# Differential attention scores: 64-row products against full-array products with zero rows

## Chip, cores and metric

The kernel runs on one core of one Trainium2 chip. The metric is the device time of one execution in microseconds (us), the median of several runs. TensorE (PE) does the matrix products, ScalarE (ACT) and VectorE (DVE) the work between them, GpSimd (POOL) small vector steps and fills, and the SP queue issues the transfers.

## The reference

One layer of a hybrid encoder block: 256 tokens, model width 2048, everything in float32. A projection feeds an mLSTM group (4 heads) and a differential attention group (8 heads); their outputs go through one output projection, and a SwiGLU feed-forward follows. Three modulation vectors per half come from `silu(c) @ w_ada`. The part that the change touches is this:

```
s = einsum('bhmqd,bhmkd->bhmqk', qb, kb) * DA_DH ** -0.5      # m: two maps of d = 64 each
allowed = k_chunk <= q_chunk                                   # chunks of 64 tokens
p = softmax(where(allowed, s, -inf))
a = p[:, :, 0] - lam * p[:, :, 1]                              # then a @ v, v of 128 per head
```

It is done in blocks of 128 queries: block 0 sees 128 keys, block 1 sees 256. Only the diagonal 128 x 128 part of a block has masked entries: its first 64 queries don't see its last 64 keys.

## The kernel before

The main stream is a list of ticks. A tick is 256 rows of K by 512 columns of a weight matrix for all 256 tokens: 12 products of 512 columns in `product` (lines 568 to 570), since each f32 operand is split into a high and a low part (`weights_hi` on ACT makes wh two ticks ahead, `weights_lo` on DVE makes wl). The raw weights come in three buffers of 1 MB, w_ada in four of 512 KB, both issued on the SP queue when a buffer comes free. The w_in sweeps come first, then w_out (wo), w_gate_up (gu) and w_down (dn).

Everything else is background work: Python generators that a planner (`Plan`) runs step by step between half ticks, in the order in which they were added, as far as free PSUM banks (four) and the booked load of DVE and ACT permit (no further step in this half tick once one of them is booked over 2.3 us). So the order of the instructions on every engine is fixed when the program is made. Its small f32 products all go through `mm` (line 216), its transposes through `tr` (line 220), ACT's instructions through `act` (line 211).

The steps around the change. `prep` (lines 715 to 746) makes the transposed q or k of four heads: squares, the norm (sclq or rstk, on DVE and, by `rsqrt_newton`, POOL lines 387 to 390), rotary products, 8 transposes into two PSUM banks, and the copy to a tile of a pool of 31 slabs (128 x 1024 f32): qT or kT, where the partitions 0 to 63 hold map 0 and 64 to 127 map 1. `attend` (lines 752 to 796), for each head: four score products with 64 partitions each, every one followed by a product of an identity matrix with the 128-column mask bmask (bf16) that adds -1e30 to the masked entries; then row maxima on DVE (line 769), a scaling on POOL (line 771), the exponentials on ACT, the difference of the two maps on DVE, transposes. `attend_values` and `finish_attention` follow. `ml_scores` (lines 910 to 958) is the same kind of step of the mLSTM group: products L and qk of 128 partitions, with a mask product of the same form. `ada_use` issues the products gv for the modulation.

Of the kernel before, what the change touches and what calls it, by code (L numbers as in the profile page):

```python
# [12 lines left out]
BF16 = mybir.dt.bfloat16  # L13
# [5 lines left out]
P = 128  # L19
D = 2048  # L20
NEG = -1.0e30
# [59 lines left out]
class Work:  # L81
    """Background work in steps; a step follows the one before it by at least a tick."""

# [6 lines left out]
class Plan:  # L90
    """Interleaves the steps of background work with the ticks of the main matrix products."""

# [72 lines left out]
def tile_block(ctx, tc, x, c, pos, par, w_ada, w_in, w_gt, w_out, w_gu, w_dn, out):  # L165
# [9 lines left out]

# [1 line left out]
    def fs(ap):  # L177
# [25 lines left out]
    def act(o, a, func, bias=None, scale=None, accum=None):  # L203
        kw = {}
        if bias is not None:
            kw["bias"] = bias
        if scale is not None:
            kw["scale"] = scale
        if accum is not None:
            kw["accum_out"] = accum  # L210
        nc.scalar.activation(o, a, func, **kw)  # L211
        n = sum(y is not None and not isinstance(y, float) for y in (bias, scale, accum))
        plan.a += fs(o) / 1200 + 0.07 + 0.09 * n
# [9 lines left out]
    def slab(name, dt=F32):  # L223
        return sl.tile([P, 1024], dt, name=name, tag="slab")
# [4 lines left out]
    def const(shape, name, dt=F32):  # L229
        return cp.tile(shape, dt, name=name)  # L230
# [3 lines left out]

# [1 line left out]
    part = const([P, NPAR - 256], "part")  # L236
# [21 lines left out]

# [1 line left out]
    ones = const([P, P], "ones")  # L260
# [13 lines left out]
    for i in range(2):  # L274
# [10 lines left out]
                            fill=NEG, base=0, channel_multiplier=1)  # L285
    bmask = const([P, P], "bmask", BF16)
    nc.gpsimd.memset(bmask[:], 0.0)
    nc.gpsimd.memset(bmask[0:64, 64:128], NEG)
    junk = const([P, 512], "junk", BF16)
# [7 lines left out]

# [1 line left out]
    items = []  # L299
# [176 lines left out]

# [1 line left out]
    ticks = []  # L478

    def visit(accname, first, last, acts, src, name, halves, ready=(), done=None):  # L480
        """halves: list of (kb, half) in the order of K; acts(kb) gives (hi, lo)."""
        for n, (kb, h) in enumerate(halves):
            ticks.append(dict(acc=accname, start=first and n == 0, stop=last and n == len(halves) - 1,
                              act=acts, kb=kb, h=h, src=src, name=name, ready=ready,
                              done=done if n == len(halves) - 1 else None, split=None, mid=None))
# [62 lines left out]
    def acc_tile(acc, k):  # L548
        """The accumulator of token tile k; those that are drained one by one have tiles of their own."""
        if acc in apart and k == 1:  # L550
            return apart[acc][:]
        return tok(accs[acc], k)
# [19 lines left out]
    def products(i, half):  # L572
        """Half of a tick; the two ticks that end a group with "split" go token tile by token tile."""
        t = ticks[i]
        if t["split"] is None:
            for k in range(2):
                product(i, half, k)
        else:
            first = i - t["split"]
            for j in range(2):  # L580
                product(first + half, j, t["split"])
        if half == 1 and t["split"] != 0:
            for n in range(i - (t["split"] or 0), i + 1):
                del wtiles[n]

# [1 line left out]
    ropet = {}  # L587
# [71 lines left out]

# [1 line left out]
    proj = {}  # L661
# [30 lines left out]

# [1 line left out]
    sclq = const([P, 2, 16], "sclq")  # L694
# [20 lines left out]
    def prep(nm, g):  # L715
        t = proj[(DQ if nm == "q" else DK)[g]]
        dst = (sclq if nm == "q" else rstk)[:, :, g * 8:(g + 1) * 8]
        tmp = sm.tile([P, 2, 16], F32, name=f"rs{nm}{g}", tag="rs", bufs=3)
        xx, b = tmp[:, :, 0:8], tmp[:, :, 8:16]
        yield 0  # L720
        sq = slab(f"sq{nm}{g}")
        act(sq[:], t[:], AF.Square)
        yield 0
        red(xx, sq.rearrange("p (t m d) -> p t m d", t=2, d=64), ALU.add)
        ts(xx, xx, 1.0 / 64, EPS, ALU.mult, ALU.add)
        rsqrt_first(dst, b, xx)
        rsqrt_newton(dst, b, xx)
        if nm == "q":
            nc.gpsimd.tensor_scalar(dst, dst, 0.125, None, op0=ALU.mult)
            rope_products(nm, t)  # L730
        else:
            yield 0
            v = t.rearrange("p (t m d) -> p t m d", t=2, d=64)
            for k in range(2):
                tt(v[:, k], v[:, k], dst[:, k].unsqueeze(2).to_broadcast([P, 8, 64]), ALU.mult)
            yield 0
            rope_products(nm, t)
        yield 2
        pts = [misc(f"tp{nm}{g}{half}") for half in range(2)]
        for half in range(2):  # L740
            transposes4(pts[half], t, half)
        yield 0
        o = (qT if nm == "q" else kT)[g] = slab(f"{nm}T{g}")
        for half in range(2):
            act(tok(o, half), pts[half][:], AF.Copy, scale=None if nm == "q" else wqk[:, 0:1])
        plan.rel(2)
# [5 lines left out]
    def attend(h):  # L752
# [3 lines left out]
        blocks = []  # L756
        for t in range(2):
            ke = 128 * (t + 1)
            for m in range(2):
                pr = slice(m * 64, m * 64 + 64)  # L760
                o = sc[m][:, t * 128:t * 128 + ke]
                mm(o, qT[g][pr, hh * 256 + t * 128:hh * 256 + t * 128 + 128], kT[g][pr, hh * 256:hh * 256 + ke],
                   True, False)
                mm(o[:, t * 128:], identb[:], bmask[:], False, True, passes=1)
                blocks.append((t, m, o))
# [78 lines left out]

# [1 line left out]
    cw = par_("cw").rearrange("p (t j) -> p t j", t=8)  # L846
# [177 lines left out]

# [1 line left out]
    def gate_rows(s, rows, name):  # L1026
# [41 lines left out]
    def turn(stage, heads):  # L1068
        """The last products of w_out and the first of w_gate_up go token tile by token tile; this is what lies between."""
        if stage == 0:  # L1070
# [31 lines left out]

# [1 line left out]
    fpart = {}  # L1104
# [74 lines left out]

# [1 line left out]
    spans = {}  # L1181
# [54 lines left out]

    # how many quarters of w_ada each span of ticks takes: (first tick, last tick, items)
    loads = []
# [13 lines left out]

# [1 line left out]
    plan.t = 3.2  # L1254
# [74 lines left out]

# [1 line left out]
    pending = []  # L1331
# [48 lines left out]
class Lazy:  # L1380
    """A generator that is made when its first step runs; that step needs no bank before it."""

# [84 lines left out]
```

## Time and profile before

| | |
|---|---|
| runs (us) | 1249.21, 1253.47, 1253.92; median 1253.47 |
| span of the profiled execution, first to last instruction | 1246.5 us (its device time is not printed) |
| mean granted TensorE clock | 0.993 |
| PE busy | 1224.0 us, 98% |
| DVE, ACT, POOL busy | 65%, 47%, 9% |
| DMA | 313.84 MB, mean 252 GB/s |
| score products (64 records) and mask products (32) of the eight heads | between 254.3 and 383.8 us |

The span is the time from the first to the last instruction of one execution. An f32 product shows as two records on PE. The end of a record is modelled, and records overlap; what a product takes of the stream is read from the start of one record to the start of the next. PEld is TensorE's weight load, PEclk the granted clock as a share of full speed.

### The profile page before, as it was taken

Reading aid. Unit: us, or ns where it says so; the run is one execution under the profiler, and the core shown is the slowest. Engines: PE = TensorE matmul, PEld = TensorE weight load, DVE = VectorE, ACT = ScalarE, POOL = GpSimd, SP = SyncE. Lnnn points to the kernel's source line nnn. Section 1 sums busy time; section 2 is a strip of 40 time slices with the busy share of each in tenths; the row PEclk is TensorE's granted clock in tenths of the full one; section 3 lists DMA queues with packets and bytes.
Section 4 is the critical chain, followed back from the end, with each engine's and each line's share of the span. In section 5 each row is a group of like instructions: output and inputs, shape, how many; then the busy total and the mean of one; then the engine's idle time right before and its main releaser. Section 6 shows DMA issues by size and latency. Waiting matters only on the chain.

```text
span 1246.5 us, 15450 instructions
## 1 busy us (share of the span) xinstructions
PE 1224.0 (98%) x5858; PEld 963.2 (77%) x5858; DVE 815.9 (65%) x1064; ACT 587.4 (47%) x817; POOL 112.2 (9%) x249
## 2 busy tenths in 40 slices
PE   6999999999999999999999999999999999999998
PEld 2667877667778788788888888888888878888886
DVE  2657976557667998777988986555445454545453
ACT  3654444446646644765434454434344443434332
POOL 1010221200302412011100000000000000000000
PEclk9999999989999999999999999999999999999999
DMA  8889997746755989698998856555555545646461
GB/s 332 300 299 349 343 377 282 281 151 249 256 219 194 330 331 353 264 341 302 354 352 332 309 181 218 201 176 200 188 183 197 183 169 195 220 169 223 165 251 54
DMA packets 63260, 313.84 MB, mean 252 GB/s; under 512 B 6993, under 2 KB 7377, under 8 KB 41169
## 3 DMA queue, kind: packets, MB, share of 16 engines
q1 hardware_dynamic: 63186, 312.86, 69.1%
q8 instruction: 46, 0.75, 0.2%
q14 instruction: 28, 0.23, 0.1%
HBM read 310.73 MB, written 2.10 MB: 251 GB/s over the span
## 4 chain that ended last, share of the span: by engine, by line
PE 95%; DMA 2%; DVE 1%; ACT 1%; issue 0%; SPq 0%; POOL 0%; ACTq 0%
PE gv L216 3%; PE sc L216 2%; DMA ada<-in_w_ada_dram 2%; PE acc('dn', 0)_8051 L570 2%; PE acc('dn', 0)_8051 L568 2%; PE acc('dn', 2)_8853 L570 2%; PE acc('dn', 2)_8853 L569 2%; PE acc('dn', 1)_8473 L570 2%; PE acc('dn', 1)_8473 L569 2%; PE acc('dn', 0)_8051 L569 2%; PE acc('dn', 2)_8853 L568 2%; PE acc('dn', 1)_8473 L568 2%; PE apart('dn', 3)_9234 L570 1%; PE apart('dn', 3)_9234 L569 1%; PE acc('dn', 3)_9233 L570 1%; PE acc('dn', 3)_9233 L569 1%
## 5 line engine op out<-in xcount | busy, mean ns | idle before, releaser
L181 DVE TENSOR_TENSOR wl<-r,wh 128x1024 fp32r<-128x1024 f32 x392 | 474.4, 1222 | 252.0 <-ACT wh L211 250.6
L211 ACT ACTIVATE wh<-r 128x1024 fp32r<-128x1024 f32 x392 | 410.3, 1058 | 414.6 <-DMA r<-in_w_gu_dram 64.7
L185 DVE SCALAR_TENSOR_TENSOR ada<-ada,silc 128x1024 f32<-128x1024 f32 x120 | 144.7, 1218 | 0.0
L376 POOL TENSOR_TENSOR modc<-part,gsum 128x2 f32<-128x2 f32 (+1 forms) x34 | 24.5, 722 | 396.5 <-DVE ada L185 277.7
L216 PE MATMUL gv<-ada,early 128*32 128x256 f32 x576 | 47.1, 420 | 4.6 <-DMA ada<-in_w_ada_dram 4.4
L216 PEld LDWEIGHTS gv<-ada,early 128*32 128x32 f32 x576 | 13.3, 112 | 30.5 <-issue 20.7
L568 PE MATMUL acc('dn', 0)_8051<-wh,aTh 128*128 128x512 f32 x88 | 35.9, 408 | 0.0
L378 POOL TENSOR_TENSOR modc<-modc,gsum 128x2 f32<-128x2 f32 (+1 forms) x58 | 30.9, 533 | 46.8 <-DVE ada L185 43.4
L570 PE MATMUL acc('dn', 0)_8051<-wh,aTl 128*128 128x512 f32 x88 | 34.3, 390 | 0.0
L569 PE MATMUL acc('dn', 0)_8051<-wl,aTh 128*128 128x512 f32 x88 | 34.3, 389 | 0.0
L568 PE MATMUL acc('dn', 1)_8473<-wh,aTh 128*128 128x512 f32 x88 | 34.2, 389 | 0.0
L569 PE MATMUL acc('dn', 1)_8473<-wl,aTh 128*128 128x512 f32 x88 | 34.2, 389 | 0.0
L570 PE MATMUL acc('dn', 1)_8473<-wh,aTl 128*128 128x512 f32 x88 | 34.2, 389 | 0.0
L568 PE MATMUL acc('dn', 2)_8853<-wh,aTh 128*128 128x512 f32 x88 | 34.2, 389 | 0.0
L569 PE MATMUL acc('dn', 2)_8853<-wl,aTh 128*128 128x512 f32 x88 | 34.2, 389 | 0.0
L570 PE MATMUL acc('dn', 2)_8853<-wh,aTl 128*128 128x512 f32 x88 | 34.2, 389 | 0.0
L181 DVE TENSOR_TENSOR hl<-hx,hh 128x512 fp32r<-128x512 f32 (+1 forms) x18 | 11.4, 632 | 26.7 <-ACT hh L211 26.6
L211 ACT ACTIVATE hx<-pt,modc,gcol 128x256 f32<-128x256 f32 (+1 forms) x36 | 17.4, 534 | 16.8 <-PE pt L220 11.7
L211 ACT ACTIVATE gr<-gv 128x256 f32<-128x256 f32 x18 | 6.9, 383 | 34.5 <-PE gv L216 34.5
L216 PE MATMUL sc<-kT,qT 64*128 64x128 f32 (+1 forms) x64 | 20.2, 397 | 0.0
L211 ACT ACTIVATE aTh<-at 128x512 fp32r<-128x512 f32 x22 | 11.9, 595 | 17.2 <-PE at L220 17.2
L569 PEld LDWEIGHTS acc('dn', 0)_8051<-wl,aTh 128*128 128x128 f32 x88 | 16.5, 188 | 4.2 <-issue 1.0
(987 smaller groups left out, 3041.6 us busy)
## 6 DMA issues: line engine op xcount, KB each, us to landing
ada<-in_w_ada_dram SPq DMA_DIRECT2D x192, 512.0 KB, 5.6
r<-in_w_gu_dram SPq DMA_DIRECT2D x76, 1024.0 KB, 5.1
r<-in_w_dn_dram SPq DMA_DIRECT2D x44, 1024.0 KB, 4.8
r<-in_w_in_dram SPq DMA_DIRECT2D x36, 1024.0 KB, 7.1
r<-in_w_out_dram SPq DMA_DIRECT2D x16, 1024.0 KB, 7.4
r<-in_w_in_dram SPq DMA_DIRECT2D x24, 512.0 KB, 5.9
r<-in_w_gu_dram SPq DMA_DIRECT2D x24, 512.0 KB, 5.2
x<-in_x_dram SPq DMA_DIRECT2D x4, 512.0 KB, 5.8
```

Source lines behind the costliest of these rows:

```text
L181: nc.vector.tensor_tensor(o, a, b, op=op)
L185: nc.vector.scalar_tensor_tensor(out=o, in0=a, scalar=s, in1=b, op0=op0, op1=op1, accum_out=accum)
L211: nc.scalar.activation(o, a, func, **kw)
L216: nc.tensor.matmul(o, l, r, start=start, stop=stop, **kw)
L376: nc.gpsimd.tensor_tensor(o, parts[0], parts[1], op=ALU.add)
L378: nc.gpsimd.tensor_tensor(o, o, y, op=ALU.add)
L568: nc.tensor.matmul(o, ah[:, s], wh[:, r], start=t["start"] and j == 0, stop=False)
L569: nc.tensor.matmul(o, ah[:, s], wl[:, r], start=False, stop=False)
L570: nc.tensor.matmul(o, al[:, s], wh[:, r], start=False, stop=t["stop"] and j == 1)
```

## The change

`bmask` becomes 256 columns wide: the 128-column mask twice. In `prep`, q is kept in two tiles, one for each map, 128 partitions each: POOL fills the other map's 64 partitions with zeros, and ACT copies the map's own 64 partitions from PSUM (four copies of 64 x 512 instead of two of 128 x 512). k stays as it is. In `attend`, one mask product of 256 columns per bank is issued first and starts the group; block 1 (256 keys) then lies in columns 0 to 255 and block 0 in columns 256 to 383 of the bank, so that the mask's columns 128 to 383 are the two diagonals. The four score products follow with all 128 partitions and add to it, block 1 first. The rest of the diff takes comments out.

```diff
-    bmask = const([P, P], "bmask", BF16)
+    bmask = const([P, 2 * P], "bmask", BF16)
     nc.gpsimd.memset(bmask[:], 0.0)
-    nc.gpsimd.memset(bmask[0:64, 64:128], NEG)
+    for y in range(2):
+        nc.gpsimd.memset(bmask[0:64, y * P + 64:y * P + 128], NEG)
...
-        o = (qT if nm == "q" else kT)[g] = slab(f"{nm}T{g}")
-        for half in range(2):
-            act(tok(o, half), pts[half][:], AF.Copy, scale=None if nm == "q" else wqk[:, 0:1])
+        if nm == "q":
+            o = qT[g] = [slab(f"qT{g}_{m}") for m in range(2)]
+            for m in range(2):
+                nc.gpsimd.memset(o[m][64 - 64 * m:128 - 64 * m, :], 0.0)
+            for half in range(2):
+                for m in range(2):
+                    r = slice(m * 64, m * 64 + 64)
+                    act(tok(o[m], half)[r], pts[half][r], AF.Copy)
+        else:
+            o = kT[g] = slab(f"kT{g}")
+            for half in range(2):
+                act(tok(o, half), pts[half][:], AF.Copy, scale=wqk[:, 0:1])
         plan.rel(2)
...
-        for t in range(2):
+        for m in range(2):
+            mm(sc[m][:, 128:384], identb[:], bmask[:], True, False, passes=1, skip_group_check=True)
+        for t, off in ((1, 0), (0, 256)):
             ke = 128 * (t + 1)
             for m in range(2):
-                pr = slice(m * 64, m * 64 + 64)
-                o = sc[m][:, t * 128:t * 128 + ke]
-                mm(o, qT[g][pr, hh * 256 + t * 128:hh * 256 + t * 128 + 128], kT[g][pr, hh * 256:hh * 256 + ke],
-                   True, False)
-                mm(o[:, t * 128:], identb[:], bmask[:], False, True, passes=1)
+                o = sc[m][:, off:off + ke]
+                mm(o, qT[g][m][:, hh * 256 + t * 128:hh * 256 + t * 128 + 128], kT[g][:, hh * 256:hh * 256 + ke],
+                   False, True, skip_group_check=True)
                 blocks.append((t, m, o))
```

## Rows read from the trace of the kernel before

**Rows 1.** The page: busy time by engine, and the chain that ended last.
```profile
PE 1224.0 (98%) x5858; PEld 963.2 (77%) x5858; DVE 815.9 (65%) x1064; ACT 587.4 (47%) x817; POOL 112.2 (9%) x249
PE 95%; DMA 2%; DVE 1%; ACT 1%; issue 0%; SPq 0%; POOL 0%; ACTq 0%
```
**Rows 2.** Stretches: length, busy PE PEld DVE ACT POOL, granted clock, DMA share, GB/s.
```profile
265.00:272.00 7.00, 7.00 (x20) 4.39 (x20) 4.64 (x14) 2.08 (x8) 1.32 (x2) 0.53 0.01 2
361.00:367.00 6.00, 6.00 (x28) 3.37 (x27) 3.72 (x10) 2.21 (x4) 0.20 (x1) 1.00 0.59 199
410.00:420.00 10.00, 9.34 (x45) 7.23 (x44) 10.00 (x17) 8.31 (x14) 0.00 (x0) 1.00 0.97 344
```
**Rows 3.** PE in order of time around head 0: start, length, what.
```profile
253.79 0.39 PE L569 MATMUL acc('in', 7, 4)_2233<-wl,hh 128*128 128x512 f32 x1
254.01 0.39 PE L570 MATMUL acc('in', 7, 4)_2233<-wh,hl 128*128 128x512 f32 x1
254.33 0.48 PE L216 MATMUL sc<-kT,qT 64*128 64x128 f32 x2
254.75 0.23 PE L216 MATMUL sc<-bmask,identb 128*128 128x128 bf16 x1
254.91 0.49 PE L216 MATMUL sc<-kT,qT 64*128 64x128 f32 x2
...
256.94 0.47 PE L568 MATMUL acc('in', 7, 4)_2233<-wh,hh 128*128 128x512 f32 x1
257.25 0.39 PE L569 MATMUL acc('in', 7, 4)_2233<-wl,hh 128*128 128x512 f32 x1
```
**Rows 4.** PE in order of time around a group of ml_scores.
```profile
324.97 0.39 PE L570 MATMUL acc('in', 4, 4)_2698<-wh,hl 128*128 128x512 f32 x1
325.20 0.59 PE L216 MATMUL L<-ml,upper 128*128 128x257 f32 x2
325.63 0.39 PE L216 MATMUL L<-ml,ones 128*128 128x129 f32 x2
325.86 0.22 PE L216 MATMUL L<-cmask,identb 128*128 128x128 bf16 x1
325.91 0.44 PE L216 MATMUL L<-ml,upper 128*128 128x129 f32 x2
...
326.25 0.87 PE L216 MATMUL qk<-cv,cv 128*128 128x128 f32 x4
326.77 0.58 PE L568 MATMUL acc('in', 4, 4)_2698<-wh,hh 128*128 128x512 f32 x1
327.19 0.40 PE L569 MATMUL acc('in', 4, 4)_2698<-wl,hh 128*128 128x512 f32 x1
```
**Rows 5.** The weight loads ahead of these two groups, in order of time.
```profile
254.33 0.29 PEld L216 LDWEIGHTS sc<-kT,qT 64*128 64x128 f32 x2 [0.35 <-ACT wh L211]
...
324.97 0.42 PEld L216 LDWEIGHTS L<-ml,upper 128*128 128x128 f32 x2
```
**Rows 6.** PE around heads 1 and 2, which run back to back.
```profile
262.03 0.48 PE L216 MATMUL sc<-kT,qT 64*128 64x128 f32 x2
...
264.76 0.48 PE L216 MATMUL sc<-kT,qT 64*128 64x128 f32 x2
...
268.80 0.78 PE L568 MATMUL acc('in', 7, 4)_2233<-wh,hh 128*128 128x512 f32 x1
...
272.31 0.39 PE L570 MATMUL acc('in', 7, 4)_2233<-wh,hl 128*128 128x512 f32 x1
```
**Rows 7.** ACT and POOL around the q copy (time order); a memset's group (busy, mean ns).
```profile
231.25 1.08 ACT L211 ACTIVATE qT<-tpq 128x512 f32<-128x512 f32 x2 [0.69 <-PE tpq L220]
233.90 1.06 ACT L211 ACTIVATE wh<-r 128x1024 fp32r<-128x1024 f32 x1 [1.56 <-issue]
...
243.14 0.21 POOL L387 TENSOR_TENSOR rsk<-rstk 128x16 f32<-128x16 f32 x1 [8.19 <-DVE rstk L192]
...
L268 POOL MEMSET early<- 128x512 f32 x1 | 0.5, 524 | 0.0
```
**Rows 8.** PE in order of time, its first products of w_ada.
```profile
12.06 2.27 PE L216 MATMUL gv<-ada,early 128*32 128x256 f32 x16 [0.95 <-DMA ada<-in_w_ada_dram]
```

## The prediction

> **What bounds the kernel now.** I read the page first. TensorE is busy 98% of the span and holds 95% of the chain that ended last [rows 1], so a microsecond taken from its stream is worth a microsecond as long as nothing else has been waiting just behind it. The stream is in program order: the main products of w_in run all the time, and the eight heads' score products are set between them, from 254 to 384 us. So I asked for the PE timeline around one head, and for comparison around a group of other small f32 products (`ml_scores`), which use all 128 rows.
>
> Between main products the start-to-start distance is 0.22 to 0.23 us [rows 3]. Head 0: the last main product before it starts at 254.01, its first score record at 254.33 (0.32, so 0.09 more than usual), the first main product after it at 256.94, the next one at 257.25 (0.31, 0.08 more than usual) [rows 3]. A head therefore puts 0.09 + 2.61 + 0.08 = 2.78 us into the stream. It holds 2 x (128 + 256) = 768 f32 columns and 4 x 128 = 512 bf16 mask columns.
>
> The comparison: 515 f32 columns for L, two 128-column masks and 384 f32 columns for qk start at 325.20, 0.23 after the main product before (no extra), the next main product starts at 326.77, and the one after it at 327.19 (0.42, 0.19 more) [rows 4]. That is 1.57 + 0.19 = 1.76 us for 899 f32 and 256 bf16 columns: more columns, a microsecond less. A mask there takes 0.05 us of the stream (325.86 to 325.91) [rows 4]; in the head, a 128-column product with its mask takes 0.58 (254.33 to 254.91) [rows 3], against 0.23 + 0.05 here. The weight loads tell why: the load for L starts at 324.97, with the product before it, 0.23 before its own; the 64-row load of a head starts at 254.33, together with its product [rows 5]. The array of the heads waits at each step between the 64-row and the 128-row form, eight times a head.
>
> The second thing in the stream is the clock. Heads 1 and 2 run back to back (262.03 and 264.76) [rows 6]. In 265 to 272 us the granted clock is 0.53 of full, so it lay at the 1.2 GHz level for nearly all of it [rows 2]; what PE did before it fell was 3 us of such head products. The other back-to-back pair, 361 to 367, kept 1.00 [rows 2].
>
> **The change part by part.** *Score products.* After the change, a head is two mask products of 256 columns and four full-array f32 products with the same 768 columns: rows of zeros cost no columns. By the comparison group: 1.76, less a 129-column product (325.63 to 325.86, 0.23), plus 256 more mask columns (2 x 0.05 = 0.10) [rows 4], makes 1.63 us. Saved per head 2.78 - 1.63 = 1.15, for eight heads 9.2 us. The bounds: at most the exit's 0.19 disappears too (1.34 a head, 10.7 us); at least each of the two masks pays the switch that a head's mask pays now, 254.75 to 254.91, 0.16 against 0.05 [rows 3, 4] (0.93 a head, 7.4 us). I take 9.2, since the comparison group has the very forms that come.
>
> Here a rule of the Trainium skill speaks against the change. The rows show 64-row products costing more than full ones [rows 3, 4]. TensorEngine Tiling, section Overview, says the opposite of half-height products: with a contraction of 64 the array can be used as two tiles, for up to twice the speed. By that, padding would give a factor away; but the same page, section Tiling Modes, says that a change of the tiling mode drains the engine, and the head changes it at every mask. The trace agrees with the second sentence; the first is a rival below.
>
> *Clock.* Head 2 took 268.80 - 264.76 = 4.04 us up to the next main product, where head 0 took 2.61 (254.33 to 256.94): 1.43 lost. The eight intervals of main products from 268.80 to 272.31 took 3.51 instead of 8 x 0.23 + 0.08 = 1.92: 1.59 lost [rows 3, 6]. Together 3.0 us. Afterwards the pair is 3.3 us of full-array products, the form of the comparison group, so I take it that this fall goes: 3.0, with bounds 0 (it falls all the same) and 6.0 (a second fall, in executions where the other pair falls too).
>
> *q kept twice.* ACT copies each half twice: two 512-column copies more per group, 1.08 us [rows 7], if 64 partitions take as long as 128. ACT stands idle 1.56 us before its next weight split at 233.90 [rows 7], which covers it for group 0; a weight split is made two ticks ahead of its products, which covers it for group 1. If both covers were gone: 2 x 1.08 = 2.2 us. The planner books about 1 us more on ACT per group and may move background steps by half a tick; the steps then meet other neighbours in the same stream, which costs or gains fractions of a us. I take nothing, and +-1 in the range.
>
> *Zero fill.* Two memsets of 64 x 1024 per group on POOL. The nearest row is 128 x 512 in 0.52 us [rows 7]; a row of twice the length makes some 1.0, 2.1 per group. They queue behind the q norm's steps and ahead of the k norm's, and POOL stands idle for 8.19 us before the latter, at 243.14 [rows 7]: hidden. PE needs the zeros only at 254.33. If that cover were gone, k's norm, its transposes and with them PE would move by 2.1 us per group. Each group also takes one more of the 31 slabs; an allocation may wait for an earlier reader. I take nothing, and 1 us in the range.
>
> *Set-up.* The mask's three memsets are longer by less than the 0.52 us of that row; PE's first products start later by this, but then wait 0.95 us for w_ada data anyway [rows 8]. Nothing. *Order of blocks.* The reductions wait for a bank's last product as now; they only come earlier.
>
> **What is late next.** After 384 us the stream is as before, 12 us earlier. DVE is the next candidate: it is busy 10.00 of 10 us in 410 to 420, where PE lost 0.66 us [rows 2]. But its load there starts with what PE delivers, and so starts earlier as well. DMA has nothing to catch up: loads are issued as buffers come free, which is earlier too.
>
> Sum: 9.2 + 3.0 = 12.2 us. The profiled execution has a span of 1246.5; its own device time is not printed. The runs are 1249.21, 1253.47 and 1253.92, so 2.7 to 7.4 lie outside that span or in executions unlike it. The sum is a difference, and I take it off the median: 1253.5 - 12.2 = 1241.3.
>
> **The rivals.** *The clock falls all the same*, there or at a new place, since the pair stays a stretch of small products. For it: it has fallen at one pair and not at the other, so it hangs on little [rows 2]. Against: no full-array stretch of small products here shows it. 1253.5 - 9.2 = 1244.3; with a further fall 1247.3, hardly to be told from no change.
> *A second fall goes*: the median run may have had one more than the profiled one (the 4.7 us between the runs leave room): 1253.5 - 15.2 = 1238.3.
> *The gain is given back*: the covers of ACT and POOL are both gone, 2.2 + 4.2 = 6.4 us: 1247.7. Against: the idle rows named above [rows 7].
> *It doesn't do what it says*: the two maps run side by side now (the rule of the Trainium skill above), and afterwards in a row. Each head would then gain nothing from the switches and stream 384 f32 columns more, at the 0.52 us of qk's 384 [rows 4]: 8 x 0.52 = 4.2 us slower, 1257.7. Against: the m = 1 product starts 0.58 us after that of m = 0, behind a mask [rows 3].
> *Slower*: a memset of the second q slab waits for that slab's last reader, and POOL, in order, holds the k norm behind it. The point is the 8.19 us of idle time at 243.14 [rows 7]: each us beyond it moves kT's transposes and with them PE. To lose 6.3 us after a gain of 12.2, the two waits must be 18.5 us beyond their cover together; at 20, 1261.3. Nothing in the profile shows a slab wait of this size on POOL.
>
> **How the numbers follow.** A measurement of this kernel can tell about 0.5%, 6.3 us, from no change. Forecast, 9 to 13 us gained: 0.58. Clock falls as before: 0.12 (1244.3), with a further fall 0.05 (1247.3). Second fall goes: 0.10 (1238.3). Given back: 0.09 (1247.7). Doesn't do what it says: 0.03. Slower: 0.03. Faster by over 6.3 (below 1247.2): 0.58 + 0.12 + 0.10 and some of the cases on the edge, 0.83. Within: 0.13. Slower: 0.04. The range: low end 1253.5 - 10.7 - 6.0 = 1236.8, with the planner's 1 us 1235.8; high end 1253.5 - 7.4 + 1 = 1247.1.
>
> **What would show it.** Right: the step from a head's first mask to the first main product after it is about 1.5 us; no extra 0.09 before it; the granted clock in 262 to 272 is 1.00; ACT and POOL rows of the fill with PE undisturbed around 231 to 254. Wrong: a record of sc with the same spacing as now, PE waiting for POOL or ACT ahead of a head, or new stretches of a clock of 0.5 between 231 and 400. The forecast fails if the spans differ by less than 9 us while the heads are as short as I say: then the gain was lost behind 384 us.

## The result, and the profile after

| | before | after |
|---|---|---|
| device time, median (us) | 1253.38 (1249.21 to 1253.92) | 1237.44 (1235.34 to 1238.58) |
| profiled execution: span (us) | 1246.5 | 1236.0 |
| mean granted TensorE clock in it | 0.993 | 0.996 |
| ratio of the times | | 0.9881, 95% interval 0.9862 to 0.9900 |

The changed kernel is 15.9 us faster. Its profiled execution took 1237.84 us, 1.84 more than its span; with the same margin the profiled execution of before took about 1248.3, well below the median of its kernel.

The page of the changed kernel, busy time by engine and the chain that ended last (before: [rows 1]):

```profile
PE 1213.9 (98%) x5842; PEld 961.8 (78%) x5842; DVE 815.3 (66%) x1064; ACT 589.2 (48%) x821; POOL 115.8 (9%) x254
PE 95%; DMA 2%; DVE 1%; ACT 1%; issue 0%; SPq 0%; POOL 0%; ACTq 0%
```

PE is busy 10.1 us less and is the bound as before. The PE timeline of the changed kernel around head 0 (start, length, what; before: [rows 3]) and around heads 1 and 2 (before: [rows 6]):

```profile
255.03 0.39 PE L571 MATMUL acc('in', 7, 4)_2239<-wh,hl 128*128 128x512 f32 x1
255.26 0.39 PE L216 MATMUL sc<-bmask,identb 128*128 128x256 bf16 x2
255.49 1.47 PE L216 MATMUL sc<-kT,qT 128*128 128x256 f32 x8
256.72 0.48 PE L569 MATMUL acc('in', 7, 4)_2239<-wh,hh 128*128 128x512 f32 x1
257.03 0.39 PE L570 MATMUL acc('in', 7, 4)_2239<-wl,hh 128*128 128x512 f32 x1
...
261.75 0.39 PE L216 MATMUL sc<-bmask,identb 128*128 128x256 bf16 x2
261.98 1.47 PE L216 MATMUL sc<-kT,qT 128*128 128x256 f32 x8
263.29 0.38 PE L216 MATMUL sc<-bmask,identb 128*128 128x256 bf16 x2
```

The first mask comes 0.23 after the main product before it, with no extra. From it to the next main product there are 1.46 us, and the main product after that starts 0.31 later, 0.08 more than usual. A head puts 1.54 us into the stream instead of 2.78; in the pair the second head starts 1.54 after the first. Saved per head: 1.24, for eight heads 9.9 us.

Three stretches of the changed kernel (length, busy PE, PEld, DVE, ACT, POOL, granted clock, DMA share, GB/s): the two pairs of heads, and the step from w_out to w_gate_up (before, the first pair: [rows 2]):

```profile
260.00:268.00 8.00, 8.00 (x43) 6.69 (x42) 5.07 (x14) 6.12 (x16) 0.80 (x2) 1.00 0.52 196
354.00:358.00 4.00, 4.00 (x25) 3.54 (x24) 3.62 (x10) 1.01 (x2) 0.41 (x2) 1.00 0.63 200
...
492.00:497.00 5.00, 4.20 (x11) 3.37 (x12) 4.02 (x10) 3.07 (x7) 0.00 (x0) 0.66 0.26 110
```

The clock stays at its upper level, 2.4 GHz, at both pairs. It falls to the lower level, 1.2 GHz, for part of 492 to 497, where PE has just stood idle twice; the corresponding stretch of the execution of before, 504 to 510, shows 1.00.

Where the 10.5 us between the two spans lie can be read from the first main product of two sweeps, `in, 7` (shortly ahead of head 0) and w_out. Of before, and then of after:

```profile
252.88 0.39 PE L568 MATMUL acc('in', 7, 4)_2233<-wh,hh 128*128 128x512 f32 x1
...
406.63 0.39 PE L568 MATMUL acc('wo', 0)_3650<-wh,odh 128*128 128x512 f32 x1
```

```profile
253.88 0.39 PE L569 MATMUL acc('in', 7, 4)_2239<-wh,hh 128*128 128x512 f32 x1
...
394.70 0.39 PE L569 MATMUL acc('wo', 0)_3645<-wh,odh 128*128 128x512 f32 x1
```

At `in, 7` the changed kernel is 1.0 us late, at w_out 11.93 ahead. So 12.9 us were won between 253 and 400: 9.9 by the heads and 3.0 by the one pair whose clock fell before. Of this the late start took 1.0 and the fall at 492 to 497 took 1.6 (from the first main product of w_gate_up to that after the next idle time: 492.80 to 498.96, before 504.74 to 509.32). The late start is a fall of the clock too: in 68 to 72 us the granted clock is 0.69, where before shows 1.00. It does not belong to the change (see the table at the end of the experiments).

q's second copy and the fill, ACT and POOL in order of time (last bracket: idle before, and what ended it; before: [rows 7]), and the group of the four fills (busy, mean ns):

```profile
232.18 2.43 ACT L211 ACTIVATE qT<-tpq 64x512 f32<-64x512 f32 x4 [0.69 <-PE tpq L220]
234.82 1.06 ACT L211 ACTIVATE wh<-r 128x1024 fp32r<-128x1024 f32 x1 [0.21 <-ACT qT L211]
...
235.94 1.95 POOL L747 MEMSET qT<- 64x1024 f32 x2
244.15 0.21 POOL L388 TENSOR_TENSOR rsk<-rstk 128x16 f32<-128x16 f32 x1 [6.26 <-DVE rstk L192]
...
L747 POOL MEMSET qT<- 64x1024 f32 x4 | 3.8, 948 | 0.2
```

Both covers held: ACT's weight split is followed by another 2.88 us of idle time, and POOL still waits 6.26 us for DVE ahead of the k norm. PE's waits between 225 and 430 sum up to 0.7 us, as before.

### The profile page after: what moved, and what is told of

It is laid out like the page before. It is cut to its first block, busy times and chain, and to the rows that moved or that the text cites. A ratio compares the mean times of both kernels' runs of the same rounds, so it can differ in the third digit from the quotient of the medians.

```text
span 1236.0 us, 15433 instructions
## 1 busy us (share of the span) xinstructions
PE 1213.9 (98%) x5842; PEld 961.8 (78%) x5842; DVE 815.3 (66%) x1064; ACT 589.2 (48%) x821; POOL 115.8 (9%) x254
## 4 chain that ended last, share of the span: by engine, by line
PE 95%; DMA 2%; DVE 1%; ACT 1%; issue 0%; SPq 0%; POOL 0%; ACTq 0%
PE gv L216 3%; DMA ada<-in_w_ada_dram 2%; PE acc('dn', 0)_8046 L571 2%; PE acc('dn', 0)_8046 L569 2%; PE acc('dn', 2)_8848 L571 2%; PE acc('dn', 2)_8848 L570 2%; PE acc('dn', 1)_8468 L571 2%; PE acc('dn', 1)_8468 L570 2%; PE acc('dn', 0)_8046 L570 2%; PE acc('dn', 1)_8468 L569 2%; PE acc('dn', 2)_8848 L569 2%; PE sc L216 1%; PE apart('dn', 3)_9229 L571 1%; PE apart('dn', 3)_9229 L570 1%; PE acc('dn', 3)_9228 L571 1%; PE acc('dn', 3)_9228 L570 1%
## 5 line engine op out<-in xcount | busy, mean ns | idle before, releaser
L569 PE MATMUL acc('dn', 0)_8046<-wh,aTh 128*128 128x512 f32 x88 | 35.9, 408 | 0.0
L571 PE MATMUL acc('dn', 0)_8046<-wh,aTl 128*128 128x512 f32 x88 | 34.3, 390 | 0.0
L570 PE MATMUL acc('dn', 0)_8046<-wl,aTh 128*128 128x512 f32 x88 | 34.3, 389 | 0.0
L569 PE MATMUL acc('dn', 1)_8468<-wh,aTh 128*128 128x512 f32 x88 | 34.2, 389 | 0.0
L570 PE MATMUL acc('dn', 1)_8468<-wl,aTh 128*128 128x512 f32 x88 | 34.2, 389 | 0.0
L571 PE MATMUL acc('dn', 1)_8468<-wh,aTl 128*128 128x512 f32 x88 | 34.2, 389 | 0.0
L569 PE MATMUL acc('dn', 2)_8848<-wh,aTh 128*128 128x512 f32 x88 | 34.2, 389 | 0.0
L570 PE MATMUL acc('dn', 2)_8848<-wl,aTh 128*128 128x512 f32 x88 | 34.2, 389 | 0.0
L571 PE MATMUL acc('dn', 2)_8848<-wh,aTl 128*128 128x512 f32 x88 | 34.2, 389 | 0.0
L211 ACT ACTIVATE hx<-pt,modc,gcol 128x256 f32<-128x256 f32 (+1 forms) x36 | 17.4, 533 | 17.7 <-PE pt L220 12.9
L570 PEld LDWEIGHTS acc('dn', 0)_8046<-wl,aTh 128*128 128x128 f32 x88 | 16.5, 188 | 4.2 <-issue 1.0
```

The source lines that it names most:

```text
L569: nc.tensor.matmul(o, ah[:, s], wh[:, r], start=t["start"] and j == 0, stop=False)
L570: nc.tensor.matmul(o, ah[:, s], wl[:, r], start=False, stop=False)
L571: nc.tensor.matmul(o, al[:, s], wh[:, r], start=False, stop=t["stop"] and j == 1)
```

## Experiments

Each kernel ran beside the kernel before on the same chip; its median there is given. What differs from the kernel before, or from another one, is in the diff.

**The kernel before, once more.** No edit; its median beside it was 1252.9.

> The kernel before, unchanged, for a second profile and the spread of its executions. The profiled execution of before had a span of 1246.5 us and one clock fall among the heads (3.0 us); the runs stood at 1249 to 1254. Theory 'the clock falls at the pairs of heads, in most executions more often than in the profiled one': a profile near 1251 to 1252 of span shows a low clock at the second pair (361 to 367) or later as well, at 2.5 to 3 us each. Rival 'it is something else, such as DMA': no more stretches at the 1.2 GHz level than in the first profile, and longer waits for data instead. Ratio 1.000 by either.

It gave 1252.33 us, ratio 0.9994 (0.9977 to 1.0012). Its profile was of another kind than that of before. The two pairs, as windows, and in the second pair its second head:

```profile
264.00:272.00 8.00, 8.00 (x23) 5.22 (x23) 5.16 (x14) 2.27 (x9) 1.32 (x2) 0.57 0.12 22
363.00:371.00 8.00, 8.00 (x24) 4.94 (x24) 2.36 (x8) 0.00 (x0) 0.41 (x2) 0.57 0.39 131
```

```profile
363.50 0.50 PE L216 MATMUL sc<-kT,qT 64*128 64x128 f32 x2
...
367.66 0.78 PE L568 MATMUL acc('in', 8, 4)_3113<-wh,hh 128*128 128x512 f32 x1
```

Here the clock fell at both pairs, and the second head of the pair took 4.16 us where a head at the upper level takes 2.61 [rows 3]. In all experiments together, 57 executions of this kernel make two groups with nothing between: 22 from 1246.74 to 1250.67 with a mean granted clock of 0.992, and 35 from 1251.96 to 1255.04 with 0.987. The profile with one fall belongs to the first group (about 1248.3); this one, with two, to the second (1251.96), and so does the time of the next experiment's, also with two. So the median most likely stands for executions with two falls. Only these were profiled; for the others it is inferred from the time alone, since the mean clocks of the two groups overlap (0.988 to 0.997 and 0.985 to 0.992). The groups lie some 4.7 us apart, more than the 3.0 of one fall: both profiles with two falls also show one behind w_out (1.6), which the profile with one does not.

**q kept twice, nothing else.** The q part of the diff as in the change; each product takes its map's 64 rows, and the masks stay as they were. Against the kernel before:

```diff
-                mm(o, qT[g][pr, ...], kT[g][pr, ...],
+                mm(o, qT[g][m][pr, ...], kT[g][pr, ...],
                    True, False)
                 mm(o[:, t * 128:], identb[:], bmask[:], False, True, passes=1)
```

> Only the preparation is changed: q in two tiles, the other map's rows filled with zeros, four ACT copies for two; the score products read the old 64 rows of these tiles, and the masks stand as before. Theory 'the fill and the copies are covered': 1253 +- 2 us, the heads at 2.78 us each. Rival 'the covers are too thin': 2 to 6 us slower, PE waiting around 231 to 254 and 319 to 345.

1252.98 us, 1.0008 (0.9992 to 1.0024). The copies and the fill cost nothing that can be measured, and the clock fell at both pairs again (from 265 and from 364).

**Full-array products, the four masks apart.** Rows of zeros as in the change; each product is followed by its own mask of 128 columns, as before. Against the changed kernel:

```diff
-            mm(sc[m][:, 128:384], identb[:], bmask[:], True, False, ...)
...
-                o = sc[m][:, off:off + ke]
+                o = sc[m][:, t * 128:t * 128 + ke]
                 mm(o, qT[g][m][:, ...], kT[g][:, ...],
-                   False, True, skip_group_check=True)
+                   True, False)
+                mm(o[:, t * 128:], identb[:], bmask[:, 0:128], False, True, passes=1)
```

> All 128 rows with zeros, but the four masks stand apart, 128 columns each, behind their product, in the old order. Theory 'what costs is the change between the 64-row and the 128-row form': there is none left, so a head takes 1.5 to 1.6 us and the time is that of the changed kernel, 1237 to 1239 us. Rival 'a mask product behind an f32 product costs 0.16 us whatever its form' (0.11 more than in the comparison group): 4 x 0.11 = 0.4 us a head more, 1241 us.

1238.51 us, 0.9898 (0.9878 to 0.9918). PE around its first pair:

```profile
262.57 0.38 PE L216 MATMUL sc<-kT,qT 128*128 128x128 f32 x2
262.79 0.22 PE L216 MATMUL sc<-bmask,identb 128*128 128x128 bf16 x1
262.85 0.44 PE L216 MATMUL sc<-kT,qT 128*128 128x128 f32 x2
...
264.27 0.44 PE L216 MATMUL sc<-kT,qT 128*128 128x128 f32 x2
```

A mask between full-array products takes 0.06 of the stream, where one between 64-row products takes 0.16 [rows 3], and the heads of a pair are 1.70 apart, a little over the 1.5 to 1.6 expected. Rows of zeros alone bring nearly the whole gain; merging the masks brings the last 0.2 per head (1.67 to 1.46 us from a single head's first record to the next main product).

**Only the masks merged and first.** No zeros: q is kept once and each product takes its 64 rows, as before. Against the kernel before, with the mask tile of 256 columns from the change:

```diff
+        for m in range(2):
+            mm(sc[m][:, 128:384], identb[:], bmask[:], True, False, ...)
-        for t in range(2):
+        for t, off in ((1, 0), (0, 256)):
...
                 pr = slice(m * 64, m * 64 + 64)
-                o = sc[m][:, t * 128:t * 128 + ke]
+                o = sc[m][:, off:off + ke]
                 mm(o, qT[g][pr, ...], kT[g][pr, ...],
-                   True, False)
-                mm(o[:, t * 128:], identb[:], bmask[:], False, True, passes=1)
+                   False, True, skip_group_check=True)
```

> Only the masks are moved: q and k as before, 64 rows for each product, but one mask of 256 columns per bank goes first, so that four 64-row products follow each other and the form changes twice a head and not eight times. Theory 'the change of the form costs': 1.54 + 2 x 0.1 = 1.7 us a head, some 1239 us. Rival 'a 64-row product cannot have its weights loaded ahead, each pays about 0.2 us': 0.2 + 2 x 0.42 + 2 x 0.63 = 2.3 us a head, 1243 to 1244 us. Rival 'the two maps run side by side once nothing stands between them': 384 columns' worth instead of 768, about 1.0 to 1.1 us a head, 1234 us. In the last case, two rows of different maps start within less than 0.1 us of each other.

1235.33 us, 0.9871 (0.9848 to 0.9895): below the changed kernel. PE around its head 0:

```profile
254.60 0.39 PE L571 MATMUL acc('in', 7, 4)_2234<-wh,hl 128*128 128x512 f32 x1
254.83 0.39 PE L216 MATMUL sc<-bmask,identb 128*128 128x256 bf16 x2
255.16 0.92 PE L216 MATMUL sc<-kT,qT 64*128 64x256 f32 x8
256.01 0.50 PE L569 MATMUL acc('in', 7, 4)_2234<-wh,hh 128*128 128x512 f32 x1
```

The two masks with the change of form behind them take 0.33 (0.23 in the changed kernel), but the eight records of the products take 0.85 instead of 1.23 us. With 0.10 on the way out a head is 1.28 us. That is less than the 1.7 us of the first expectation and near the last one, two maps side by side. The prediction had counted the 768 columns one after the other, and here they don't pass so. The clock stayed at its upper level at both pairs.

**The changed kernel and this one on one chip.** Both unchanged.

> The changed kernel, unchanged, beside the version with only the masks merged and first. Expected 1237.5 us (1236.0 to 1239.5), 0.988 of the kernel before. A head 1.46 us from mask to main product, pairs 1.54 us apart, granted clock 1.00 at the pairs.

> Only the masks merged and issued first; q kept once, products of 64 rows. The head was 1.28 us here against 1.54 us of the changed kernel, so eight heads make 8 x 0.26 = 2.1 us: expected 1235.3 us, 1.5 to 2.5 below the changed kernel. Rival: the 2.1 us between the two were a matter of chips and of other falls of the clock; then the two agree within 0.7 us. The pairs should keep the granted clock at 1.00 in either case.

1236.04 (1235.34 to 1237.92) and 1234.00 us (1233.26 to 1235.51), beside 1252.46 of the kernel before: 2.0 us apart, 8 x 0.26 = 2.1 expected. The medians agree with the heads of the two traces, although single executions overlap; the table below shows the same 2.0 without the falls of the clock elsewhere.

**Map by map.** As above, but both products of map 0 ahead of both of map 1.

```diff
-        for t, off in ((1, 0), (0, 256)):
-            ke = 128 * (t + 1)
-            for m in range(2):
-                pr = slice(m * 64, m * 64 + 64)
+        for m in range(2):
+            pr = slice(m * 64, m * 64 + 64)
+            for t, off in ((1, 0), (0, 256)):
+                ke = 128 * (t + 1)
```

> As the version with only the masks merged and first, but both products of map 0 ahead of both of map 1. Theory: products of different maps run side by side only where they are neighbours in the stream; here only the middle two are (128 columns of map 0 with 256 of map 1), so of 768 columns 640 have to pass one after the other instead of 384: a head gets longer by up to 256 f32 columns, 0.3 to 0.5 us, and the kernel 2.4 to 4 us slower, 1237.7 to 1239.5 us. Rival: the short head of that version comes only from the form changes that went with the masks; then the order of the four products does not matter and the time stays at 1235.3 us.

1233.75 us beside the 1234.00 above: no difference, so the theory of neighbours fell in this form. A row merges records that follow each other; in windows shorter than a record they part, and they come in twos. First the version above, t by t, then this one, map by map:

```profile
254.03 0.49 PE L216 MATMUL sc<-kT,qT 64*128 64x256 f32 x2
254.35 0.38 PE L216 MATMUL sc<-kT,qT 64*128 64x256 f32 x2
254.57 0.39 PE L216 MATMUL sc<-kT,qT 64*128 64x128 f32 x4
```

```profile
255.40 0.49 PE L216 MATMUL sc<-kT,qT 64*128 64x256 f32 x2
255.72 0.39 PE L216 MATMUL sc<-kT,qT 64*128 64x256 f32 x2
255.93 0.39 PE L216 MATMUL sc<-kT,qT 64*128 64x128 f32 x4
```

In both, two records of 256 columns start at one time, two more 0.32 later, and the four of 128 columns follow 0.21 to 0.22 after those. In the second kernel the four records of 256 columns are two of map 0 and two of map 1, with map 0's 128-column product between them in the program; still all four start before any record of 128 columns does. So map 1's products passed map 0's second product. The second record of the first two starts 7 ns behind the first in the one kernel and 13 ns in the other, where two more records stand ahead of it in the program. It remained open whether the halves of the array do this, or whether products of 64 rows are merely cheaper.

**All on one half.** Masks merged and first, t by t, but map 1's products take map 0's rows, so the second map's scores are left out and products of the same size stand in their place.

```diff
-                pr = slice(m * 64, m * 64 + 64)
+                pr = slice(0, 64)
```

> As the version with only the masks merged and first, but the score products of map 1 take map 0's rows too (partitions 0 to 63 of q and k), so map 1's scores are those of map 0: a part of the computation is replaced by another of the same size. Theory: products of different row halves run side by side (384 columns at four cycles each, 0.64 us, instead of 768, 1.28 us); all on one half they must pass one after the other, a head takes about 0.85 + 0.4 to 0.6 us from first product to main product, and the kernel gets 3 to 5 us slower than that version, 1237 to 1239 us. Rival: products of 64 rows are simply cheaper than products of 128 rows, one after the other; then nothing changes (1234 to 1235 us, 0.85 us).

1241.02 us (1239.70 to 1241.50); the version without this edit gave 1234.87 on this chip: 6.2 slower, somewhat more than the 3 to 5 expected. PE around head 0:

```profile
255.04 0.39 PE L216 MATMUL sc<-bmask,identb 128*128 128x256 bf16 x2
255.36 1.57 PE L216 MATMUL sc<-kT,qT 64*128 64x256 f32 x8
256.86 0.50 PE L569 MATMUL acc('in', 7, 4)_2234<-wh,hh 128*128 128x512 f32 x1
```

The steps between single records of 256 columns, first in the changed kernel (128 rows), then here (64 rows, one half), from windows shorter than a record:

```profile
255.49 0.38 PE L216 MATMUL sc<-kT,qT 128*128 128x256 f32 x1
255.71 0.38 PE L216 MATMUL sc<-kT,qT 128*128 128x256 f32 x1
```

```profile
255.68 0.38 PE L216 MATMUL sc<-kT,qT 64*128 64x256 f32 x1
255.90 0.38 PE L216 MATMUL sc<-kT,qT 64*128 64x256 f32 x1
```

The clock around the pair:

```profile
260.00:270.00 10.00, 10.00 (x49) 7.71 (x49) 6.59 (x18) 7.90 (x20) 1.32 (x2) 1.00 0.48 165
```

The same eight records take 1.50 us instead of 0.85. So 64-row products are not cheaper one after the other (1.23 in full form); it is the two halves that run side by side, worth 0.65 a head, 5.2 us. Nor are they dearer: a record of 256 columns follows the one before it after 0.22 us in the full form and on one half, and on two halves two start in each 0.22. The 0.27 between 1.50 and 1.23 lie at the two ends, where the form changes: 0.32 instead of 0.22 from the first record to the second, and 0.20 instead of 0.03 from the last one to the main product. About 1 us of the 6.2 lies outside the heads (5.0 in the table below).

**Masks of 64 rows too.** Masks merged and first, one on each half, so that PE changes its form only at the ends of a head. wmask holds 1/64 for the first 64 queries, and every row of the mask has the same entries, so that 64 rows add up to the mask.

```diff
-        nc.gpsimd.memset(bmask[0:64, y * P + 64:y * P + 128], NEG)
+        nc.gpsimd.memset(bmask[:, y * P + 64:y * P + 128], NEG)
+    wmask = const([P, P], "wmask", BF16)
+    nc.gpsimd.memset(wmask[:], 0.0)
+    nc.gpsimd.memset(wmask[:, 0:64], 1.0 / 64)
...
-            mm(sc[m][:, 128:384], identb[:], bmask[:], ...)
+            pr = slice(m * 64, m * 64 + 64)
+            mm(sc[m][:, 128:384], wmask[pr, :], bmask[pr, :], ...)
```

> As the version with only the masks merged and first, but the mask products have 64 rows as well, one on either half (weights of 1/64 for the first 64 queries, a mask with the same entries in all rows). Theory: the two masks then run side by side (one length of 256 bf16 columns, 0.11 us, instead of two) and the change of form between masks and products is gone, or stands ahead of the masks instead: a head 1.28 -> 1.10 to 1.18 us, 0.8 to 1.4 us less in all, 1233 to 1234 us. Rival: masks and products are serial on the shared bank or in the change of form anyway: 1.28 us, no difference. The times alone can hardly tell 1 us; the step from mask to main product in the trace does.

> The version with only the masks merged and first once more, for the comparison on one chip: 1234 to 1235.5 us, a head 1.28 us.

1233.97 and 1234.87 us (beside 1252.51): 0.9 apart, which the times can't tell from nothing; the table below shows 1.45. PE of the first kernel, head 0 and the second heads of the two pairs:

```profile
254.27 0.39 PE L574 MATMUL acc('in', 7, 4)_2237<-wh,hl 128*128 128x512 f32 x1
254.59 0.28 PE L216 MATMUL sc<-bmask,wmask 64*128 64x256 bf16 x2
254.71 0.82 PE L216 MATMUL sc<-kT,qT 64*128 64x256 f32 x8
255.46 0.50 PE L572 MATMUL acc('in', 7, 4)_2237<-wh,hh 128*128 128x512 f32 x1
...
261.34 0.57 PE L216 MATMUL sc<-bmask,wmask 64*128 64x256 bf16 x2
261.65 0.92 PE L216 MATMUL sc<-kT,qT 64*128 64x256 f32 x8
...
351.58 0.27 PE L216 MATMUL sc<-bmask,wmask 64*128 64x256 bf16 x2
351.69 0.82 PE L216 MATMUL sc<-kT,qT 64*128 64x256 f32 x8
```

ACT in the same trace:

```profile
261.39 0.20 ACT L211 ACTIVATION_READ_ACCUMULATOR pm<-sc,st,sclq 128x1 f32 x1
```

Both masks together now take 0.12, and the change of form stands ahead of them: the first mask comes 0.32 after the main product, 0.09 more than usual. From there to the next main product 0.87 us pass, so a single head is 0.87 + 0.09 + 0.11 = 1.07 us instead of 1.28. In the first pair the second head's masks take 0.31 up to its products, in the second pair 0.11. In the first, one of the two masks starts only at 261.64, 0.05 behind the end of ACT's last instruction on the scores of an earlier head (261.39 to 261.59): most likely it waits for that PSUM bank, and not for a change of form. Both this and the version before it beat the changed kernel.

**Each head's products twice.** The changed kernel, with a second set of the same masks and products ahead of the first; the repeated set adds nothing to the result.

```diff
+        for m in range(2):
+            nc.tensor.matmul(sc[m][:, 128:384], identb[:], bmask[:], start=True, stop=False, ...)
+        for t, off in ((1, 0), (0, 256)):
+            ke = 128 * (t + 1)
+            for m in range(2):
+                nc.tensor.matmul(sc[m][:, off:off + ke], qT[g][m][:, ...], kT[g][:, ...], start=False, stop=True, ...)
```

> The changed kernel with each head's two mask products and four full-array products issued twice (the first set is overwritten by the second, so it adds nothing to the result). Work added: 8 x 1.4 to 1.54 us = 11 to 12 us, about 1249 us. A pair of heads is then about 6 us of small products, longer than the 5.5 us of the kernel before. Theory: the clock falls at a pair of the kernel before because its products of 64 rows, each waiting for a change of form, keep the array less busy; full-array products do not let it fall, so the pairs keep 1.00. Rival: any stretch of small products of some 5 us lets the clock fall; then a granted clock of about 0.5 stands right after the pairs' start, as before, and up to 6 us more are lost: 1252 to 1255 us.

1249.30 us, 13.3 more than the changed kernel on this chip, of which 8 x 1.53 = 12.2 are the added products. The clock over the two pairs:

```profile
255.00:275.00 20.00, 20.00 (x116) 16.45 (x115) 10.92 (x25) 9.87 (x24) 2.43 (x3) 1.00 0.42 152
350.00:380.00 30.00, 30.00 (x160) 25.54 (x159) 22.00 (x49) 15.55 (x44) 2.33 (x7) 1.00 0.63 241
```

A pair is 6.04 us of small products here (263.75 to 269.79), longer than a pair of before, and the clock stays up. Length alone does not let it fall.

**One stretch in every trace.** Whole executions mix the heads with falls of the clock elsewhere. In 68 to 72 us the granted clock is 0.57 to 0.71 in six of the thirteen traces, and sweep `in, 9` then takes 8.3 to 8.5 us instead of 6.9. Behind w_out it falls in five, and the first sweep of w_gate_up then takes 9.0 to 9.1 us instead of 7.4 to 7.5. Both come and go between traces of one and the same kernel. From the first main product of `in, 7` to that of w_out there are all eight heads and neither of these falls:

| kernel | us, by trace |
|---|---|
| before; once more | 153.75; 156.72 |
| q kept twice | 156.81 |
| changed; once more | 140.82; 140.82 |
| full-array products, masks apart | 142.60 |
| only the masks merged and first, three traces | 138.84; 138.85; 138.83 |
| map by map | 138.84 |
| all on one half | 143.87 |
| masks of 64 rows too | 137.38 |
| each head's products twice | 153.08 |

Traces of one kernel agree within 0.02 us here, where the clock does the same at the pairs. The second fall of before costs 2.97, and before with two falls is 15.90 behind the changed kernel: the 15.9 of the medians.

## Why the prediction was right, and where it was off

*The result* lies in the range, 3.9 us below the forecast of 1241.3; the case that came is the rival "a second fall goes" (1238.3).

*Score products.* The mechanism held: the array did lose its time in eight changes of form. The saving was 9.9 us, not 9.2. The term that was off is the way out: the sum took 0.19 from the comparison group [rows 4], the heads have 0.08. Without this difference the forecast head of 1.63 would be 1.52; it is 1.54.

*Clock.* The fall did go. The step that failed is its size: 3.0 us came from a profiled execution with one fall, but were taken off a median that most likely stands for executions with two. 9.9 + 2 x 3.0 = 15.9, the gain measured, and the stretch with all heads gives 15.90 between a profiled execution with two falls and the changed kernel. Against the profiled execution with one fall the prediction said 12.2, and 12.9 were won between 253 and 400. That the medians agree with this stretch so closely is in part luck, since the falls at 68 us and behind w_out come and go (1.4 and 1.6 us each). The rule would have been to ask first whether the profiled execution is one like the median: its span and the runs shown left room for it, and the prediction put that into a rival with a chance of 0.10.
What lets the clock fall is narrowed down, not settled. It fell at five of the six pairs in the three profiled executions with 64-row products and full-array masks in turn, and at none of twenty pairs in the ten of other kernels: full-array products with masks between them, full-array sets of 6 us, 64-row products in a row, on two halves or on one. Length alone does not do it, nor does the 64-row form in pairs of up to 3.65 us; the alternation is what the five have in common. But before each fall PE had done 2.9 to 3.7 us of a pair, and no stretch of 64-row products without the alternation was longer than that, so the cause stays open.

*Side by side.* The prediction held that rows speak against this rule of the Trainium skill (TensorEngine Tiling, section Overview: up to twice the speed with a contraction of 64) since the m = 1 product started 0.58 us behind that of m = 0. That is true of the kernel before, with a mask between them. It was wrong to carry it over to products with no mask between: there the pace is 1.50 / 0.85 = 1.8 times that of one half, and twice between the ends (two records in each 0.22 us). Nor does a 64-row product itself cost more than a full one, though the prediction read its rows so; what the head paid for was the change of form on either side of it. The trace bears the rule out, with what the same page of the Trainium skill says in the section Tiling Modes (a change of mode drains the engine, tiles operate independently) as the likely reason why the kernel before got nothing from it. The rival built on it, that padding would cost 4.2 us, was wrong for that kernel. But it points at the better change: moving the masks alone brings 8 x (2.78 - 1.28) = 12.0 us and the two falls, 18.0 in sum, 17.6 measured on one chip (1252.51 - 1234.87). Rows of zeros then take back 2 us of it.

*q kept twice, zero fill, set-up.* Nothing, as forecast, shown by its own run. The fill is 0.95 us per piece (forecast 1.0), the covers were left with 6.26 us on POOL. The rivals that stood on them ("given back", "slower") had nothing behind them.

*What is late next.* Nothing up to w_out: no new wait of PE. Between the 12.9 us won there and the 10.5 us of the spans lie 2.4; the late start (1.0) and the fall of the clock at 492 (1.6) account for them up to 0.2.

## What to carry to other kernels

Small matrix products between large ones are priced by the start-to-start steps around a group of the same form, and products of different array forms should stand together, not in turn. When a contraction of 64 leaves half the array empty, look first at what stands between the products of the two halves before filling the half with zeros: here one reordering, with no added data, gave more than the padding. And before a difference is taken off a median, ask whether the profiled execution is one like the median: its span beside the times of the other runs is the first sign. And where the clock comes and goes, compare one stretch of the traces, from the same product to the same product, rather than whole executions.

## What the hardware showed beside this

- Products on the two row halves start together even when the program has another product of the first half between them (map by map, 1233.75 against 1234.00 us, records in twos).
- An f32 record of 256 columns takes 0.22 us of the stream with 64 rows as with 128; on one half the eight records take 1.50 us against 1.23 in full form only because of the change of form at their ends.
- Four ACT copies of 64 x 512 take 2.43 us where two of 128 x 512 took 1.08 [rows 7]: half the partitions save nothing. POOL's fill of 64 x 1024 takes 0.95 us, that of 128 x 512 took 0.52 [rows 7]: the row length counts there too.
- The granted clock can fall while PE is busy 7.00 of 7 us [rows 2], and from one execution to the next it does so or not: in three traces of the kernel before and of q kept twice it fell at five of six pairs, some 3.0 us each.
